# Rotary key of a latent-attention block: the low parts of its weights laid in the free columns beside the high parts, two matmul passes in place of three

## The chip, the cores and the metric

The kernel runs on one core of one Trainium2 chip. The metric is the device time of one execution in microseconds (us), as the median of several runs. Engines are named as the profile names them: PE is TensorE (matmuls), PEld its weight loads, DVE is VectorE, ACT is ScalarE, POOL is GpSimd, SP is SyncE, whose queue starts the DMAs.

## What is computed

The reference is a two-layer encoder over 512 tokens of width 1024. Each layer has three mixers side by side (latent attention, a gated linear recurrence in both directions, windowed attention), a gated merge, cross-attention and a gated feed-forward part. The change touches the shared rotary key of the latent attention alone. Cut to what matters:

```python
h = _rmsnorm(x, g_mix[l])
(a_cq, a_ckv, a_kr, b_q, b_ff, b_fb, ...) = _split_cols(h @ w_in[l], IN_SPLITS)   # a_kr: 32 columns

def _rope(x, pos):                       # x1, x2: the two halves of the 32 columns
    return concatenate([x1 * cos - x2 * sin, x1 * sin + x2 * cos])

k_rope = broadcast(_rope(a_kr, pos))     # one key of 32 columns, the same for all 8 heads
```

## The kernel before

**Precision.** All large products are kept near float32 by splitting each operand into a high part, rounded to the type fp32r, and a low part, the rest. `mm3` (line 153) issues three matmuls for a product of a weight block and an activation chunk: high by high, high by low, low by high. The fourth product, low by low, is left out.

**Weights.** All weights come as one stream of blocks of 128 x 128, four blocks to a unit. `_fetch` (L112) starts the DMA of a unit five ahead, `_part` splits a unit: ACT writes the high parts `whi` (L120), DVE subtracts and writes the low parts `wlo` (L121). `_next` does this so that a unit is parted two units before PE reads it (`LOOK = 3`). `blk` hands out the next block as a pair (high, low). Each tile `whi` and `wlo` holds 128 x 512 elements and there are five of each.

**The rotary key.** `mla_pre` makes a list of steps; the step `key` (line 574) multiplies the 1024 input features with a block of 128 columns, in eight chunks of 128 features (`kc`), so eight blocks, two units, 24 matmuls into one PSUM bank. The 32 wanted columns stand in the block twice, each time as themselves and as their two halves swapped: `[kr, krs, kr, krs]`. Two DVE instructions (L581) multiply the result by the tables of cosines and sines; the step `rope` (`turned`) sums the pairs by one matmul with a constant matrix of zeros and ones (`C_SWAP`) and splits the key.

**Where it stands.** The recurrence `hgrn` goes over eight heads, and its last two rounds carry the latent attention's first steps as filler for PE: in round `i == 6` the steps `ckv0`, `ckv1`, `key`, in that order, and in round 7 `cq0`, `nckv`, `cq1`, `rope`, `cq2`, `ncq`. Ahead of `key` in the same round stand the scores of head 6 (`hgrn_scores`), and in the round before `decay(heads[7])` was issued: some twenty DVE instructions for each direction (`hgrn_decay`, L410 to L463), part of them on ACT and POOL. Right after `key`, PE has the scores of head 7 (144 small matmuls), then `cq0`.

**What sets the order.** The tile framework orders each engine's instructions when the program is built: it puts waits on semaphores where a tile's region was written or read by another engine, and it may set an instruction behind later written ones of its engine. On the chip each engine's queue runs in that fixed order. Every layer runs the same code.

Of the kernel before, what the change touches and what calls it, by code (L numbers as in the profile page):

```python
# [9 lines left out]
F32 = mybir.dt.float32  # L10
# [6 lines left out]
P = 128  # L17
D = 1024
# [3 lines left out]
KC = D // P  # L22
# [22 lines left out]
C_M, C_ID, C_SWAP, C_BONE, C_SM = 0, 512, 640, 768, 896  # L45
# [3 lines left out]
def _consts():  # L49
    c = np.zeros((P, CTOT), np.float32)  # L50
    inv = (10000.0 ** (-np.arange(16, dtype=np.float32) / np.float32(16))).astype(np.float32)
    ang = np.arange(T, dtype=np.float32)[:, None] * inv[None, :]
    cos = np.cos(ang).T.astype(np.float32)
    sin = np.sin(ang).T.astype(np.float32)
    cs = np.concatenate([cos, cos, -sin, sin], 0)
    one = np.ones((64, T), np.float32)
    rope = np.stack([np.concatenate([one, cs], 0), np.concatenate([cs, one], 0)])
    t = np.arange(T)
    c[:, C_M:C_M + T] = (t % 16 != 0)
    c[:, C_ID:C_ID + P] = np.eye(P)  # L60
    p = np.arange(P)
    c[:, C_SWAP:C_SWAP + P] = (p[:, None] == p[None, :]) | (p[:, None] == (p[None, :] ^ 32))
    c[:, C_BONE:C_BONE + P] = ((p[:, None] // 64) == (p[None, :] // 64))
    j = np.arange(16)
    for i in range(4):
        n = 1 << i
        c[:, C_SM + 16 * i:C_SM + 16 * i + 16] = (j % n != 0)
        c[:, C_SM + 64 + 16 * (3 - i):C_SM + 80 + 16 * (3 - i)] = (j % n != 0)
    same = (p[:, None] // 32) == (p[None, :] // 32)
    mf = (~same) | (p[:, None] <= p[None, :])  # L70
    mb = (p[:, None] % 32) >= p[None, :]
    m = np.concatenate([mf, mb], 1).astype(np.int32)
    return c, m, rope


class _K:
# [479 lines left out]
    def mla_pre(self, l, h):  # L556

        nc = self.nc
        st = {"ckv": [], "cq": [], "acc": {}}

        def latent(nm, off, c):
            def run():
                if nm == "ckv" and c == 0:
                    st["rope"] = [self.t2(), self.t2()]
                    for e in range(2):
                        nc.sync.dma_start(st["rope"][e], self.roped[e])
                b, = self.projs("w_in", l, np.arange(D), [off + c * P + np.arange(P)], h)
                t = self.t2()
                nc.scalar.activation(t, b, AF.Copy)
                st["acc"][nm] = self.sumsq(t, st["acc"].get(nm))  # L570
                st[nm].append(t)
            return run

        def key():

            kr = O_KR + np.arange(32)
            krs = O_KR + np.concatenate([np.arange(16, 32), np.arange(16)])
            b, = self.projs("w_in", l, np.arange(D), [np.concatenate([kr, krs, kr, krs])], h)
            u = st["u"] = self.t2()
            for e, a in ((0, slice(64, 128)), (1, slice(0, 64))):  # L580
                nc.vector.tensor_tensor(u[a], b[a], st["rope"][e][a], op=ALU.mult)  # L581

        def norm(nm, n, g):
            def run():
                r = self.rstd(st["acc"][nm], n * P)
                st["n", nm] = [(self.t2(F32R), self.t2(F32R)) for _ in range(n)]
                self.norm_split(st[nm], V_N * l + g, r, st["n", nm])
            return run

        def turned():  # L590
            krr = self.bank()
            self.mm(krr, self.cst[:, C_SWAP:C_SWAP + P], st["u"], True, True)
            ktab = self.c8([P, 4, T], F32R)
            kt = st["kt"] = [(ktab[:, 0], ktab[:, 1]), (ktab[:, 2], ktab[:, 3])]
            for e in range(2):
                a = slice(64, 128) if e == 0 else slice(0, 64)
                self.split(kt[e][0][a], kt[e][1][a], krr[a])

        self.mst = st
        res = dict(key=key, rope=turned, nckv=norm("ckv", 2, V_GKV), ncq=norm("cq", 3, V_GQ))  # L600
        res.update({f"ckv{c}": latent("ckv", O_CKV, c) for c in range(2)})
        res.update({f"cq{c}": latent("cq", O_CQ, c) for c in range(3)})
        return res
# [519 lines left out]
def _layout(inp):  # L1123
    f = {k: np.asarray(v) for k, v in inp.items()}
    xT = np.ascontiguousarray(f["x"][0].T.reshape(KC, P, T).transpose(1, 0, 2))
    memT = np.ascontiguousarray(f["mem"][0].T.reshape(KC, P, M).transpose(1, 0, 2))
    cols = []
    for l in range(NL):
        for n in ("g_mix", "g_x", "g_mem", "g_ffn", "a_gq", "a_gkv"):
            cols.append(_cols(f[n][l]))  # L1130
        cols.append(np.tile(f["b_gout"][l], 2)[:, None])
        cols.append(np.tile(f["c_sink"][l][None], (P, 1)))
    cols.append(_cols(f["g_final"]))
    cols.append(_cols(f["b_lb"]))
    vec = np.ascontiguousarray(np.concatenate(cols, 1))
    assert vec.shape == (P, VTOT), vec.shape
    rel = np.arange(384)[None, :] - P - np.arange(P)[:, None]
    ext = np.concatenate([f["rel_bias"], np.full((1, 8), -1e30, np.float32)], 0)
    idx = np.where(np.abs(rel) <= 128, _t5_bucket(rel), 32)
    bias = np.ascontiguousarray(ext[idx].transpose(2, 0, 1))  # L1140
    cst, msk, rope = _consts()
    return dict(xT=xT, memT=memT, vec=vec, cst=cst, msk=msk, rope=rope, bias=bias)
# [37 lines left out]
```

## Time and profile before

| | |
|---|---|
| median of 3 runs | 2372.4 us (2371.82 to 2373.35) |
| the profiled execution's own time | 2371.25 us |
| its span in the profile | 2369.5 us |
| PE busy | 2336.9 us, 99% of the span |
| DVE busy | 1469.8 us, 62% |
| ACT busy | 1187.3 us, 50% |
| POOL busy | 167.8 us, 7% |

How to read it: the span goes from the first to the last instruction, the own time adds what lies around it. PE's busy time is the share of the span in which a matmul was under way; back-to-back matmuls overlap, so the mean duration of one is longer than the distance from one to the next. In a timeline row the first number is the start, the second how long the row's instructions took together, and a bracket at the end gives the idle time before and who ended it.

### The profile page before, as it was taken

The page shows a single profiled execution, that of the slowest core. Times are in us where ns is not written, and L with a number is a line of the kernel's source. Part 1 is how long each engine was busy: PE and PEld are TensorE (multiplying, and loading weights), DVE is VectorE, ACT ScalarE, POOL GpSimd, SP SyncE. Part 2 cuts the span into 40 slices and gives each one's busy share as a digit, 9 for nine tenths or more (in the row PEclk, how much of TensorE's full clock was granted, in tenths as well). Part 3 has the DMA queues.
Part 4 walks back from the last instruction along what each step waited for, and adds up shares of the span by engine and source line. Part 5 has one row for each costly group of instructions (what it writes and reads, how often), then busy time and mean ns, then how long its engine had stood idle before and what let it go on. Part 6 is the DMA issues. An engine that isn't in the chain of part 4 may idle for free.

```text
span 2369.5 us, 34666 instructions
## 1 busy us (share of the span) xinstructions
PE 2336.9 (99%) x12934; PEld 1901.6 (80%) x12934; DVE 1469.8 (62%) x2753; ACT 1187.3 (50%) x2162; POOL 167.8 (7%) x165
## 2 busy tenths in 40 slices
PE   9999999999999999999999999999999999999998
PEld 7877778777888888888887777777788888888886
DVE  8876756566756555355577866666657575553553
ACT  7766566556545433233367656655555454332332
POOL 1332300000000000000013322000000000000000
PEclk9999999999999999999999999999999999999999
DMA  4223233234553233333432223322345523333332
GB/s 163 86 86 94 84 96 103 80 98 134 196 148 89 80 94 98 98 96 96 130 106 87 84 69 102 98 85 91 95 140 178 147 76 94 94 98 98 96 96 76
DMA packets 133513, 246.26 MB, mean 104 GB/s; under 512 B 14816, under 2 KB 17120, under 8 KB 132960
## 3 DMA queue, kind: packets, MB, share of 16 engines
q1 hardware_dynamic: 133344, 244.05, 33.5%
q8 instruction: 101, 1.65, 0.3%
q14 instruction: 68, 0.56, 0.1%
HBM read 227.22 MB, written 16.78 MB: 103 GB/s over the span
## 4 chain that ended last, share of the span: by engine, by line
PE 85%; DVE 6%; issue 4%; POOL 2%; ACT 2%; DMA 1%; POOLq 0%; DVEq 0%; SPq 0%; ACTq 0%
PE ps L151 83%; POOL c L463 1%; PE ps L658 1%; DVE c L463 1%; DVE t L417 1%; POOL t L414 1%; DVE wlo L121 1%; DVE c L444 1%; PE ps L790 1%; DVE c L445 0%; ACT whi L120 0%; PE ps L939 0%; DMA t<-in_bias_dram 0%; DMA wraw<-in_w_dram 0%; PE ps L286 0%
## 5 line engine op out<-in xcount | busy, mean ns | idle before, releaser
L151 PE MATMUL ps<-c,whi 128*128 128x512 f32 (+1 forms) x5696 | 1733.9, 387 | 5.9 <-ACT whi L120 5.9
L151 PEld LDWEIGHTS ps<-c,whi 128*128 128x128 f32 x5696 | 1058.3, 188 | 236.8 <-issue 16.9
L151 PE MATMUL ps<-c,wlo 128*128 128x512 f32 (+1 forms) x2848 | 1096.9, 385 | 6.5 <-DVE wlo L121 6.5
L120 ACT ACTIVATE whi<-wraw 128x512 fp32r<-128x512 f32 x764 | 475.1, 629 | 817.3 <-PE ps L151 606.4
L121 DVE TENSOR_TENSOR wlo<-wraw,whi 128x512 fp32r<-128x512 f32 x764 | 526.5, 697 | 545.7 <-ACT whi L120 535.9
L151 PEld LDWEIGHTS ps<-c,wlo 128*128 128x128 f32 x2848 | 535.7, 188 | 116.2 <-DVE wlo L121 9.1
L151 PE MATMUL ps<-c,t 128*64 128x512 f32 (+6 forms) x960 | 167.5, 418 | 4.5 <-DVE smw L767 2.3
L151 PEld LDWEIGHTS ps<-c,t 128*64 128x64 f32 (+2 forms) x960 | 99.7, 167 | 55.3 <-issue 31.6
L988 DVE TENSOR_TENSOR t<-ps,t 128x512 f32<-128x512 f32 x112 | 76.3, 689 | 103.3 <-PE ps L151 103.3
L463 POOL TENSOR_TENSOR c<-c,smx 128x256 f32<-128x256 f32 x128 | 122.8, 988 | 111.0 <-DVE c L444 82.8
L414 POOL TENSOR_TENSOR t<-t,t 128x512 f32<-128x512 f32 x32 | 44.1, 1379 | 1184.4 <-ACT t L413 1169.0
L970 DVE TENSOR_TENSOR c<-ps,c 128x512 f32<-128x512 f32 x64 | 44.2, 690 | 70.1 <-PE ps L151 70.1
L463 DVE TENSOR_TENSOR c<-c,smx 128x256 f32<-128x256 f32 x128 | 81.6, 695 | 0.2
L151 PEld LDWEIGHTS ps<-c 128*32 128x32 f32 (+1 forms) x2304 | 61.2, 120 | 12.2 <-PE ps L151 5.3
L151 PE MATMUL ps<-c 128*32 128x32 f32 (+3 forms) x2304 | 69.3, 218 | 0.2
L180 ACT ACTIVATE c<-ps 128x512 fp32r<-128x512 f32 (+2 forms) x78 | 42.7, 547 | 39.9 <-PE ps L151 38.9
L181 DVE TENSOR_TENSOR c<-ps,c 128x512 fp32r<-128x512 f32 (+2 forms) x78 | 49.3, 632 | 20.8 <-ACT c L180 20.4
L441 ACT ACTIVATE t<-t 128x512 f32<-128x512 f32 x32 | 20.1, 629 | 79.7 <-DVE t L440 79.7
L417 DVE TENSOR_TENSOR_SCAN t<-cst,t 128x512 f32<-128x512 f32 x32 | 39.0, 1220 | 23.7 <-POOL t L414 23.7
L181 DVE TENSOR_TENSOR c<-t,c 128x512 fp32r<-128x512 f32 (+1 forms) x84 | 51.6, 634 | 3.3 <-ACT c L180 3.3
L180 ACT ACTIVATE c<-t 128x512 fp32r<-128x512 f32 (+1 forms) x84 | 48.0, 581 | 8.6 <-DVE t L982 3.5
L645 ACT ACTIVATE t<-ps,sm 128x512 f32<-128x512 f32 x64 | 43.5, 687 | 12.6 <-DVE sm L643 12.5
(144 smaller groups left out, 1788.2 us busy)
## 6 DMA issues: line engine op xcount, KB each, us to landing
wraw<-in_w_dram SPq DMA_DIRECT2D x764, 256.0 KB, 2.6
gate<-t SPq DMA_DIRECT2D x32, 256.0 KB, 2.3
t<-gate SPq DMA_DIRECT2D x32, 256.0 KB, 3.9
c<-in_xT_dram SPq DMA_DIRECT2D x16, 256.0 KB, 5.5
gate_b<-t SPq DMA_DIRECT2D x16, 256.0 KB, 3.4
t<-gate_b SPq DMA_DIRECT2D x16, 256.0 KB, 3.8
t<-in_bias_dram SPq DMA_DIRECT2D x16, 192.0 KB, 3.6
c<-in_memT_dram SPq DMA_DIRECT2D x3, 1024.0 KB, 8.2
```

Source lines behind the costliest of these rows:

```text
L120: self.nc.scalar.activation(hi, raw, AF.Copy)
L121: self.nc.vector.tensor_tensor(lo, raw, hi.bitcast(F32), op=ALU.subtract)
L151: self.nc.tensor.matmul(o, a, b, start=start, stop=stop)
L180: nc.scalar.activation(hi, src, AF.Copy)
L181: nc.vector.tensor_tensor(lo, src, hi.bitcast(F32), op=ALU.subtract)
L414: nc.gpsimd.tensor_tensor(f, f, g, op=ALU.add)
L417: scan = lambda o, m, x: nc.vector.tensor_tensor_scan(o, m, x, 0.0, op0=ALU.mult, op1=ALU.add)
L444: tt(qd, hd["q"], f, op=ALU.mult)
L463: eng.tensor_tensor(ov, sv, ev, op=ALU.mult)
L645: nc.scalar.activation(p, s, AF.Exp, bias=nm, accum_out=sm)
L970: nc.vector.tensor_tensor(x[c], b, xold[c], op=ALU.add)
L988: self.nc.vector.tensor_tensor(t, b, r, op=ALU.mult)
```

## The change

Line numbers of the changed kernel are the same up to `key` and 7 higher behind it.

```diff
-    c[:, C_SWAP:C_SWAP + P] = (p[:, None] == p[None, :]) | (p[:, None] == (p[None, :] ^ 32))
+    c[:, C_SWAP:C_SWAP + P] = (p[:, None] % 32 == p[None, :] % 32)
...
             kr = O_KR + np.arange(32)
             krs = O_KR + np.concatenate([np.arange(16, 32), np.arange(16)])
-            b, = self.projs("w_in", l, np.arange(D), [np.concatenate([kr, krs, kr, krs])], h)
+            cols = np.concatenate([kr, krs, kr, krs])
+            b = self.bank()
+            for kc in range(KC):
+                hi, lo = self.blk("w_in", l, np.arange(kc * P, (kc + 1) * P), cols)
+                nc.vector.tensor_copy(hi[:, 64:128], lo[:, 64:128].bitcast(F32))
+                for x in range(2):
+                    self.mm(b, hi, h[kc][x], kc == 0 and x == 0, kc == KC - 1 and x == 1)
```

In each of the eight blocks a DVE copy (a CAST in the lists below, L583) puts the low parts of the block's columns 64 to 127 over the high parts there. The block in `whi` then has high parts in columns 0 to 63 and low parts of the same weights in columns 64 to 127. It is multiplied with the high and the low part of the activations: two matmuls for each block, 16 in place of 24. The bank holds products of the high weights in rows 0 to 63 and of the low weights in rows 64 to 127, and the constant matrix now sums the four rows that belong to one output instead of two. The product low by low is now in the sum. The weight stream, its DMAs and its splitting are unchanged.

The program's order around the change, in the first layer (the second layer has the same rows under other numbers). `whi_3037` is the first unit of the key's weights, `whi_3055` the second, `ps_3076` the key's bank.

PE, the key's matmuls on the second unit (blocks 5 to 8), before:

```order
L151 MATMUL ps_3076<-c_44_221,whi_3055 128x512 [waits Activation_49]
L151 MATMUL ps_3076<-c_45_222,whi_3055 128x512
L151 MATMUL ps_3076<-c_44_221,wlo_3056 128x512 [waits DVE_49]
L151 MATMUL ps_3076<-c_44_221,whi_3055 128x512
L151 MATMUL ps_3076<-c_45_222,whi_3055 128x512
```

and now, to the first matmul of the scores of head 7:

```order
L151 MATMUL ps_3076<-c_44_221,whi_3055 128x512 [waits DVE_49,Activation_49]
L151 MATMUL ps_3076<-c_45_222,whi_3055 128x512
L151 MATMUL ps_3076<-c_44_221,whi_3055 128x512 [waits DVE_49]
L151 MATMUL ps_3076<-c_45_222,whi_3055 128x512
L151 MATMUL ps_3076<-c_44_221,whi_3055 128x512 [waits DVE_49]
L151 MATMUL ps_3076<-c_45_222,whi_3055 128x512
L151 MATMUL ps_3076<-c_44_221,whi_3055 128x512 [waits DVE_49]
L151 MATMUL ps_3076<-c_45_222,whi_3055 128x512
L151 MATMUL ps_3116<-c_494_2831 32x32 [waits PE_49]
```

Before, one wait for DVE's split covered the unit; now blocks 5, 6, 7 and 8 each wait for DVE on their own.

DVE, where the copies of the first unit and the first copy of the second unit stand now (the rows around them are those of before):

```order
L121 TENSOR_TENSOR wlo_3038<-wraw_2994,whi_3037 128x512 [waits DMAHW5_49,PE_49,Activation_49]
L411 TENSOR_SCALAR t_478_2768<-t_478_2768 128x512 [waits DVE_49]
L583 CAST whi_3037<-wlo_3038 128x64 [waits DVE_49]
L583 CAST whi_3037<-wlo_3038 128x64 x3
L492 COPY_PREDICATED zz_102<-msk_159,ps_2902 128x128 [waits PE_49]
...
L121 TENSOR_TENSOR wlo_3056<-wraw_3012,whi_3055 128x512 [waits DMAHW6_49,Activation_49]
L430 COPY smx_2872<-t_500_2870 128x16 [waits DVE_49]
L583 CAST whi_3055<-wlo_3056 128x64 [waits DVE_49,PE_49]
L431 TENSOR_TENSOR smx_2872<-smx_2872,t_500_2870 128x64 [waits DVE_49]
```

All four copies of the first unit follow that unit's split (L121) at once; of the second unit only the first copy does.

DVE, where the other three copies of the second unit stand, in the same queue, 21 instructions of other work later (the first ten, L431 to L396, are not shown):

```order
L463 TENSOR_TENSOR c_502_2885<-c_494_2831,smx_2872 128x256 [waits DVE_49]
L463 TENSOR_TENSOR c_502_2885<-c_494_2831,smx_2872 128x256 x3
L181 TENSOR_TENSOR c_154_825<-t_503_2894,c_153_824 128x512 [waits Activation_49]
L496 TENSOR_TENSOR c_506_2967<-zz_102 32x4x32 x4
L121 TENSOR_TENSOR wlo_3080<-wraw_3035,whi_3079 128x512 [waits DMAHW7_49,PE_49]
L121 TENSOR_TENSOR wlo_3098<-wraw_3053,whi_3097 128x512 [waits DMAHW0_49,Activation_49]
L583 CAST whi_3055<-wlo_3056 128x64 x3
L121 TENSOR_TENSOR wlo_3208<-wraw_3077,whi_3207 128x512 [waits DMAHW1_49,Activation_49]
L258 TENSOR_TENSOR t_520_3032<-t_520_3032,t_529_3073 128x512 [waits Activation_49]
```

The three copies that blocks 6, 7 and 8 wait for stand behind the end of head 7's decay (L463), the rest of head 6's scores (L496) and the splits of the next two units (the first two L121 rows), and ahead of the third.

## Rows read from the trace of the kernel before

**Rows 1.** Page, parts 1 and 2: busy us (share) xinstructions; granted clock in tenths.
```profile
PE 2336.9 (99%) x12934; PEld 1901.6 (80%) x12934; DVE 1469.8 (62%) x2753; ACT 1187.3 (50%) x2162; POOL 167.8 (7%) x165
...
PEclk9999999999999999999999999999999999999999
```

**Rows 2.** Page, part 5, costliest groups: busy, mean ns of one, idle before.
```profile
L151 PE MATMUL ps<-c,whi 128*128 128x512 f32 (+1 forms) x5696 | 1733.9, 387 | 5.9 <-ACT whi L120 5.9
...
L151 PE MATMUL ps<-c,wlo 128*128 128x512 f32 (+1 forms) x2848 | 1096.9, 385 | 6.5 <-DVE wlo L121 6.5
```

**Rows 3.** Waits of PE over the whole span: total us, times, longest us.
```profile
PE ps L151 <- DVE wlo L121: 6.5, 4, 2.3
PE ps L151 <- ACT whi L120: 5.9, 1, 5.9
PE ps L151 <- DVE t L258: 3.0, 2, 1.5
```

**Rows 4.** Timeline of PE, first layer: the key, head 7's scores, cq0.
```profile
282.19 0.62 PE L151 MATMUL ps<-c,whi 128*128 128x512 f32 x2
...
287.41 0.39 PE L151 MATMUL ps<-c,wlo 128*128 128x512 f32 x1
287.72 4.62 PE L151 MATMUL ps<-c 128*32 128x32 f32 x144
292.10 0.71 PE L151 MATMUL ps<-c,whi 128*128 128x512 f32 x2
```

**Rows 5.** Timeline of DVE, first layer, around the second key unit's split.
```profile
279.22 1.22 DVE L417 TENSOR_TENSOR_SCAN t<-cst,t 128x512 f32<-128x512 f32 x1 [1.18 <-POOL t L414]
280.36 0.67 DVE L121 TENSOR_TENSOR wlo<-wraw,whi 128x512 fp32r<-128x512 f32 x1
280.95 0.17 DVE L430 COPY smx<-t 128x16 f32<-128x16 f32 x1
281.15 0.28 DVE L431 TENSOR_TENSOR smx<-smx,t 128x64 f32<-128x64 f32 x1
...
286.86 2.16 DVE L496 TENSOR_TENSOR c<-zz 32x128 f32<-32x128 f32 x4
289.05 2.20 DVE L121 TENSOR_TENSOR wlo<-wraw,whi 128x512 fp32r<-128x512 f32 x3
...
292.48 1.41 DVE L581 TENSOR_TENSOR t<-ps,t 64x512 f32<-64x512 f32 x2
```

**Rows 6.** Timeline of DVE, first layer, behind the first key unit's split.
```profile
267.41 0.42 DVE L411 TENSOR_SCALAR t<-t 128x512 f32<-128x512 f32 x1
268.46 0.30 DVE L492 COPY_PREDICATED zz<-msk,ps 128x128 f32<-128x128 int32 x1 [0.63 <-PE ps L151]
```

**Rows 7.** Timelines of DVE and PE, second layer, the same place.
```profile
1463.31 2.20 DVE L121 TENSOR_TENSOR wlo<-wraw,whi 128x512 fp32r<-128x512 f32 x3
...
1461.99 4.62 PE L151 MATMUL ps<-c 128*32 128x32 f32 x144
```

**Rows 8.** Timeline of PE, first layer: head 6's scores and what follows.
```profile
267.12 4.30 PE L151 MATMUL ps<-c 128*32 128x32 f32 x144
271.18 0.71 PE L151 MATMUL ps<-c,whi 128*128 128x512 f32 x2
```

**Rows 9.** Chain that ended last, 280 to 300 us: start, us, what.
```profile
283.90 4.35 POOL c L463 x2
```

**Rows 10.** Stretches at the end: length, PE busy (x), PEclk, DMA share, GB/s.
```profile
2361.20:2362.70 1.50, 0.00 (x0) 1.00 0.00 0
2362.70:2364.20 1.50, 0.00 (x0) 0.55 0.98 378
```

**Rows 11.** Timeline of PE: its first matmuls, the twelfth's successor, its last ones.
```profile
5.88 1.22 PE L151 MATMUL ps<-c,whi 128*128 128x512 f32 x2 [5.88 <-ACT whi L120]
...
11.13 0.63 PE L151 MATMUL ps<-c,whi 128*128 128x512 f32 x2
...
2358.56 1.12 PE L151 MATMUL ps<-t,small 128*128 128x512 f32 x2 [0.59 <-ACT t L253]
```

## Prediction, made before the changed kernel was run

> **What bounds the kernel now.** I read the busy shares first, then the costliest groups, then PE's waits, and then the timelines of PE and DVE around the key. PE is busy 99% of the span at full granted clock [rows 1], nearly all of it in 128 x 512 matmuls on the weight stream [rows 2]. So a matmul that leaves PE's queue saves its distance to the next one, and a wait that is added to PE's queue is paid in full unless a wait further on shrinks by as much. PE's waits are few: apart from the start (5.9 us) the longest is 2.3 us, and that is for DVE's weight splits [rows 3]. DVE is busy only 62% over the span, but that is an average: from 279.22 to 293.9 us, in the stretch where the key stands, it has not one idle gap, working off head 7's decay; the first and the last row of that stretch, and the pieces that matter here, stand in [rows 5].
>
> **What is removed.** Eight matmuls a layer, those on `wlo`. The key's 24 matmuls start at 282.19 and the last starts at 287.41 [rows 4]: 5.22 us for 23 distances, 0.227 us each. 8 x 0.227 = 1.8 us a layer, 3.6 us for both. The bank, the two products with the tables, the one matmul with the constant matrix and the weight stream stay, at no cost either way: same instructions, same shapes, other numbers in them.
>
> **What is added.** Eight copies of 128 x 64 on DVE a layer. No row shows this operation. The nearest are the copy of 128 x 16, 0.17 us, and the two-input operation of 128 x 64, 0.28 us [rows 5]. The copy has the first one's operation and the second one's size; I take 0.2 us, with 0.1 and 0.28 as bounds (a negative price is excluded, since nothing is taken off DVE).
> The four copies of the first unit stand behind L411, which ends at 267.83, and ahead of a wait for PE that ended at 268.46 after 0.63 us of idle time [rows 6]. They need 0.8 us, so 0.2 us sticks out, and the next idle time takes it: DVE waits 1.18 us for POOL ahead of 279.22 [rows 5]. Their price is nothing; and PE reads this unit only at 282.19. If that idle time were gone, the price would be at most 0.8 us of DVE.
> The first copy of the second unit stands behind L430, at about 281.12, and delays all that follows on DVE by 0.2 us. Block 5 waits for it, at 282.19 + 8 x 0.227 = 284.0: hidden by almost 3 us.
>
> **The wait that decides.** The copies for blocks 6, 7 and 8 stand behind L496 and two weight splits. In the trace those splits begin at 289.05, three in 2.20 us, so two of them take 1.47 us and end at 290.52 [rows 5]. Add the 0.2 us of the first copy and 0.2 us for the copy itself: DVE delivers block 6 at about 290.95. PE wants it after ten matmuls, at 282.19 + 10 x 0.227 = 284.46. It will stand still for about 6.5 us. Nothing in DVE's queue up to there waits for PE's key, so DVE will not be later for it, nor earlier. The remaining copies follow at 0.2 us and a block lasts 0.45 us, so there is one stall, not three.
> Queued behind the stalled matmul on PE are the scores of head 7, `cq0` and everything after. The key's last matmul ends at 290.95 + 6 x 0.227 = 292.31 instead of 287.64: 4.67 us later, and the saved 1.8 us is in this number.
>
> **What comes back.** Head 7's scores take 4.38 us from their start to `cq0` [rows 4], but head 6's take 4.06 [rows 8]: in the trace they wait briefly for POOL, whose L463 ends at 288.25 [rows 9]. That wait will be over: 0.32 us back. Net 4.67 - 0.32 = 4.35 us a layer. DVE reaches the key's products (L581) at 292.48 anyway [rows 5], so they and what hangs on them are not later by more than about 1 us, and PE's next wait, 1.5 us for L258 near 322 us, is paced by PE's own matmuls ahead of it and moves along. The second layer has the same rows 1174.26 us later [rows 7], so I count everything twice: 8.7 us.
>
> **The clock.** A stall of 6.5 us has no like in the middle of this kernel. At its end it has: the last matmuls are over at 2359.7 [rows 11], the granted clock is still 1.00 up to 2362.7, and 0.55 in the next stretch, so it falls to 0.5, the 1.2 GHz level, about there, after PE has done nothing for some 3 us [rows 10]. And at the beginning the first 12 matmuls, after PE stood still for 5.88 us, take 11.13 - 5.88 = 5.25 us [rows 11], 0.44 each, where the same work takes 12 x 0.227 = 2.72 later: 2.5 us lost, at a spacing which I read as the lower level, though the page's clock row prints full clock there. By the waits in the middle alone (2.3 us at most, clock at full [rows 1, 3]) there would be no such loss and the sum would be 8.7 us; by the ends a stall that is more than twice as long as the silence before 2362.7 costs the clock too. I take the ends, and 2.5 us a layer, bounds 0 and 7.9: the upper one if the six matmuls left of the key (6 x 0.21 = 1.3 us), the whole of the scores (4.06 us more) and then another 2.5 us go at half speed.
> The Trainium skill, on the page "TensorE: Matmul & The Clock Gate", section "HAM oscillation — how this bites in real kernels", says that bursts of matmuls with waits between them start each burst at the halved clock once the waits are long enough. By that rule the sum would be the higher one; the mid-kernel waits of this trace neither confirm nor contradict it, as none is long, and the fall at the end agrees.
>
> **Sum.** Against the profiled execution's own 2371.25 us: 2371.25 + 8.7 + 2 x 2.5 = 2385.0 us. That execution lies 1.15 us below the median of the runs shown, well inside their spread. 0.2% of the time, 4.7 us, is about what a measurement of this kernel can tell from no change.
>
> **Rivals.**
> *The clock holds.* The stall is as computed, but PE restarts at full speed: 2371.25 + 8.7 = 2380.0. For it: no fall is seen between two matmuls anywhere in the span. Against it: the fall at the end.
> *The clock stays low through the scores.* The stage of 144 tiny matmuls keeps PE less occupied than the projections, and the clock may come back only in `cq0`: 2371.25 + 2 x (4.35 + 7.9) = 2395.8. For it: the trace has no row for this stage at the low clock. Against it: at full clock the same stage has never let the clock fall [rows 1].
> *The copies are in time, and it is not slower.* If DVE delivered block 6 by 284.46, only the 16 matmuls would be gone: 2371.25 - 3.6 = 2367.6. The point from which it decides is 6.5 us ahead of where the queue's order puts the copy, and DVE has no idle time between 280.36 and 290.5 to be taken out. What speaks for it is only that DVE's pace there may differ; it would have to finish 10 us of work in 3.5.
> *The stall is paid back later.* PE's longest later wait in a layer (1.5 us for L258 [rows 3]) would be shorter because DVE and ACT use the stall to get ahead. If the 1.5 us went and the clock held: 2371.25 + 2 x (4.35 - 1.5) = 2377.0. Against it: the work ahead of the L258 wait begins with a matmul result that is late by the same amount.
>
> **How the numbers follow.** Forecast, with the clock lost for a few us in one or both layers (2382 to 2388): 0.58. The clock holds: 0.20. Low through the scores: 0.12. Paid back: 0.06. Copies in time: 0.04. The range leaves out the copies in time and the edge of the outer cases: 2377 to 2396, from the paid-back case to the long low clock; the bounds of the copy's price, 0.2 us a layer, lie inside it. The copies in time (3.6 us faster) and about half of the paid-back case are within 0.2%: 0.07. Faster by more needs more than the removed matmuls are worth: 0.01. Slower: 0.92.
>
> **What would show it.** PE: 16 matmuls fewer; one wait of about 6.5 us in each layer put down to DVE's `whi` at L583, near 284.5 and 1458.7 us, inside the key; no wait of 0.3 us inside head 7's scores. DVE: the last three copies right behind two L121 rows at about 290.7. Clock: a dip in the stretch after 288 us and matmuls 0.43 apart for a few us. It is wrong if the three copies run before 285 us, if PE waits there for something else, if the rows after the stall are at full speed (then 2380), or if the waits after 295 us shrink by more than 1 us a layer.

## The result, and the profile after

The changed kernel takes 2387.21 us, the median of 5 runs (2383.16 to 2388.13), against 2372.8 us (5 runs) for the kernel before, run beside it: ratio 1.0056, 95% interval [1.0045, 1.0068]. It is slower by 14.4 us, 0.6%. The forecast was 2385.0 us, range 2377 to 2396, slower with a chance of 0.92. The prediction was right; the last sections say in which terms it was right for the right reason, and where errors met.

The profiled execution of the changed kernel took 2386.18 us, its span 2384.4 us, so it lies 14.9 us above that of before. Busy times hardly moved: PE issues 12918 matmuls, 16 fewer than in [rows 1], and is nevertheless busy for 2338.7 us, 1.8 us longer; DVE is busy for 1470.0 us, 62% as before. No share shows where 15 us went. PE's waits do (changed kernel, whole span: total us, times, longest us):

```profile
PE ps L151 <- DVE whi L583: 12.5, 2, 6.3
PE ps L151 <- DVE wlo L121: 6.0, 4, 2.3
PE ps L151 <- DVE t L258: 3.3, 3, 1.5
```

The first line is new, the others stand about as in [rows 3]. One wait of 6.3 us in each layer, for a copy at L583. Where it stands, the timeline of PE in the first layer shows (changed kernel; start, us, instruction, idle time before and who ended it), to be read beside [rows 4]:

```profile
283.23 2.43 PE L151 MATMUL ps<-c,whi 128*128 128x512 f32 x10
291.93 2.93 PE L151 MATMUL ps<-c,whi 128*128 128x512 f32 x6 [6.27 <-DVE whi L583]
294.79 4.30 PE L151 MATMUL ps<-c 128*32 128x32 f32 x144
298.84 0.71 PE L151 MATMUL ps<-c,whi 128*128 128x512 f32 x2
```

Ten matmuls, five blocks, at full speed; then 6.27 us of nothing; then the last six, which start 2.86 us before the scores, where 6 x 0.227 = 1.36 us would be their distance at the pace of the first ten. From the key's first matmul to the end of head 7's scores it is 298.84 - 283.23 = 15.61 us, where it was 292.10 - 282.19 = 9.91 us: +5.70. The second layer has the same rows, with a slower end (changed kernel, PE):

```profile
1464.62 2.43 PE L151 MATMUL ps<-c,whi 128*128 128x512 f32 x10
1473.31 2.93 PE L151 MATMUL ps<-c,whi 128*128 128x512 f32 x6 [6.26 <-DVE whi L583]
1476.17 5.53 PE L151 MATMUL ps<-c 128*32 128x32 f32 x144
1481.45 0.70 PE L151 MATMUL ps<-c,whi 128*128 128x512 f32 x2
```

In the kernel before, the same stage of the second layer begins and ends so (PE):

```profile
1456.46 0.62 PE L151 MATMUL ps<-c,whi 128*128 128x512 f32 x2
...
1466.37 0.70 PE L151 MATMUL ps<-c,whi 128*128 128x512 f32 x2
```

Here the stage takes 16.83 us instead of 9.91: +6.92. The scores themselves took 5.28 us from their start to the next matmul, in the first layer 4.05. The granted clock tells why (changed kernel, stretches of both layers, start and end in us: length, PE busy (matmuls), PEclk, DMA share, GB/s):

```profile
287.50:291.90 4.40, 0.00 (x0) 0.55 0.00 0
291.90:294.70 2.80, 2.77 (x6) 0.50 0.84 241
294.70:298.80 4.10, 4.10 (x144) 0.99 0.51 133
...
1473.30:1476.20 2.90, 2.89 (x10) 0.50 0.80 230
1476.20:1481.40 5.20, 5.20 (x144) 0.71 0.41 127
```

During the stall the clock falls to 0.50, the 1.2 GHz level. In the first layer it is back at full when the scores begin; in the second it comes back within them. The queue of DVE shows who is late (changed kernel, DVE, first layer; some rows left out), to be read beside [rows 5]:

```profile
268.80 0.49 DVE L583 CAST whi<-wlo 128x64 fp32r<-128x64 f32 x4
269.52 0.30 DVE L492 COPY_PREDICATED zz<-msk,ps 128x128 f32<-128x128 int32 x1 [0.22 <-PE ps L151]
...
282.19 0.20 DVE L583 CAST whi<-wlo 128x64 fp32r<-128x64 f32 x1
...
287.99 2.15 DVE L496 TENSOR_TENSOR c<-zz 32x128 f32<-32x128 f32 x4
290.18 1.59 DVE L121 TENSOR_TENSOR wlo<-wraw,whi 128x512 fp32r<-128x512 f32 x2
291.69 0.38 DVE L583 CAST whi<-wlo 128x64 fp32r<-128x64 f32 x3
```

The first unit's four copies run 14 us ahead of PE and go into idle time (0.63 us of it before [rows 6], 0.22 now). The second unit's first copy is also in time, its other three run at 291.69, between the second and third of the next units' splits, and PE starts again at 291.93.

The 14.9 us add up so: 1.04 us by which the key starts later (283.23 against 282.19; DVE's split of the key's first unit, which stands ahead of the first copies, already begins 1.05 us later, at 267.86 against 266.81, so this is no part of the change), 5.70 in the first layer, 1.42 between the layers (a clock fall of its own, last section), 6.92 in the second layer, -0.2 at the end. The two stages of the change give 12.6 us of it.

### The profile page after: what moved, and what is told of

It is laid out like the page before. It is cut to its first block, busy times and chain, and to the rows that moved or that the text cites. A ratio compares the mean times of both kernels' runs of the same rounds, so it can differ in the third digit from the quotient of the medians.

```text
span 2384.4 us, 34644 instructions
## 1 busy us (share of the span) xinstructions
PE 2338.7 (98%) x12918; PEld 1902.2 (80%) x12918; DVE 1470.0 (62%) x2769; ACT 1187.9 (50%) x2162; POOL 169.7 (7%) x165
## 4 chain that ended last, share of the span: by engine, by line
PE 84%; DVE 7%; issue 4%; ACT 2%; POOL 2%; DMA 1%; SPq 0%; DVEq 0%; POOLq 0%; ACTq 0%
PE ps L151 82%; PE ps L665 1%; DVE c L463 1%; POOL c L463 1%; DVE t L417 1%; DVE wlo L121 1%; POOL t L414 1%; DVE c L444 1%; PE ps L797 1%; DVE c L445 0%; DMA c<-in_memT_dram 0%; DVE c L496 0%; ACT whi L120 0%; PE ps L946 0%; DMA t<-in_bias_dram 0%
## 5 line engine op out<-in xcount | busy, mean ns | idle before, releaser
L121 DVE TENSOR_TENSOR wlo<-wraw,whi 128x512 fp32r<-128x512 f32 x764 | 526.5, 697 | 556.0 <-ACT whi L120 542.9
L463 POOL TENSOR_TENSOR c<-c,smx 128x256 f32<-128x256 f32 x128 | 124.8, 1003 | 111.2 <-DVE c L444 82.8
L463 DVE TENSOR_TENSOR c<-c,smx 128x256 f32<-128x256 f32 x128 | 80.3, 685 | 0.2
```

Source lines behind the costliest of these rows:

```text
L121: self.nc.vector.tensor_tensor(lo, raw, hi.bitcast(F32), op=ALU.subtract)
L463: eng.tensor_tensor(ov, sv, ev, op=ALU.mult)
```

## The experiments

The runs come in two sets, each on a chip of its own and each beside the kernel before (medians 2373.3 and 2373.09 us). Theory: DVE's queue place makes PE wait 6.3 us, and the clock makes it dearer. Rivals: the copies cost by the work that they are; the stall alone is the price; the matmuls saved are worth nothing.

**The stall filled.** Behind the fifth block of each key, and so ahead of the wait for the sixth, 26 matmuls whose result nobody reads:

```diff
+                if kc == 4:
+                    spare = self.bank()
+                    for _ in range(26):
+                        self.mm(spare, hi, h[kc][0], True, True)
```

> The changed kernel, with 26 more matmuls of 128x512 between block 5 and block 6 of the key, into a bank that nothing reads: work of 26 x 0.227 = 5.9 us a layer laid into the stall of 6.3 us. Theory (PE stands still there for a copy that DVE delivers late, and the clock falls because PE stands still): the matmuls cost nothing, the stall shrinks to some 0.4 us, no matmul behind it runs at the lower clock, and the time falls below that of the changed kernel: 2371.25 + 2 x 4.35 = 2380, plus at most 1.4 us where the clock falls elsewhere; 2380 to 2382. Rival (PE is simply slower by something else, the clock has no part in it): at least as slow as the changed kernel, 2386 to 2388, or, were there no stall to fill, 2386 + 11.8 = 2398.

Measured: 2380.82 us, median of 4 runs (2379.39 to 2385.58); ratio 1.0036 [1.0023, 1.005]. That is 6.4 us faster than the changed kernel by the medians of two sets, with 52 matmuls more; by the two ratios it is 0.0020, or 4.7 us, and their intervals overlap a little. Its size is better read from the stage. PE in the first layer, and its stretches:

```profile
284.75 8.32 PE L151 MATMUL ps<-c,whi 128*128 128x512 f32 x36
293.86 1.65 PE L151 MATMUL ps<-c,whi 128*128 128x512 f32 x6 [0.78 <-DVE whi L583]
295.44 4.30 PE L151 MATMUL ps<-c 128*32 128x32 f32 x144
299.50 0.70 PE L151 MATMUL ps<-c,whi 128*128 128x512 f32 x2
```

```profile
290.00:293.00 3.00, 3.00 (x14) 1.00 0.00 0
293.00:295.40 2.40, 1.62 (x7) 1.00 0.43 139
295.40:299.50 4.10, 4.10 (x146) 1.00 0.68 206
```

The last six matmuls still wait for L583, and PE does nothing useful in the same stretch, but the clock stays at 1.00 and they go at 1.58 us instead of 2.86. The stage takes 299.50 - 284.75 = 14.75 us, +4.84 on before; the second layer's takes 14.74. The wait is not quite the same one: PE goes on 9.11 us after the key's start (293.86 - 284.75), in the changed kernel 8.70 us, as DVE came 0.41 us later here.

So the extra time in the changed kernel can be taken apart. The clock takes 2.86 - 1.58 = 1.28 us from the last six matmuls in each layer, and 5.28 - 4.05 = 1.23 us from the scores of the second: 3.8 us. Without it the two stages are 5.70 - 1.28 = 4.42 and 6.92 - 2.51 = 4.41 us longer than before: that is the wait less the matmuls saved, 8.8 us. The difference of the medians from the kernel with the stall filled, 6.4 us, is larger than these 3.8; only one execution of each kernel has rows, and where the rest lies isn't shown. (The profiled execution of this run, 2385.58 us, is the slowest of the four; it lost clock at two other places, near 222 and 1403 us.)

**No copies at all.** The line with the copy is taken out, so the two passes see high parts alone and the products with the low weights are left out:

```diff
-                nc.vector.tensor_copy(hi[:, 64:128], lo[:, 64:128].bitcast(F32))
```

> The changed kernel without its eight copies a layer: two passes on the high parts alone, so the product of the low weights is left out. It shows what the removal of the 16 matmuls is worth by itself. Theory: nothing or little, since PE now reaches the scores of head 7 at 285.9 instead of 287.7, and the same chain of DVE, ACT and POOL (its L463 ended at 288.25 in the kernel before) releases them: a wait of about 2.1 us for POOL in place of 0.3; 2372 to 2373. Rival (each matmul that leaves the queue saves its 0.227 us, as the forecast priced it): 2372.4 - 3.6 = 2368.8.

Measured: 2372.65 us, 11 runs (2368.26 to 2375.89); ratio 0.9996 [0.9987, 1.0005]. The whole loss is gone, but no gain can be told from zero, though 16 matmuls are gone; the 3.6 us that they would be worth lie just outside the interval. PE in the two layers:

```profile
283.52 3.79 PE L151 MATMUL ps<-c,whi 128*128 128x512 f32 x16
287.24 0.76 PE L151 MATMUL ps<-c 128*32 128x32 f32 x28
288.42 4.03 PE L151 MATMUL ps<-c 128*32 128x64 f32 x116 [0.42 <-DVE c L463]
292.20 0.70 PE L151 MATMUL ps<-c,whi 128*128 128x512 f32 x2
...
1457.76 3.79 PE L151 MATMUL ps<-c,whi 128*128 128x512 f32 x16
1463.23 0.36 PE L151 MATMUL ps<-c 128*32 128x32 f32 x10 [1.38 <-POOL c L463]
1463.86 4.05 PE L151 MATMUL ps<-c 128*32 128x64 f32 x116 [0.27 <-POOL c L463]
1467.66 0.70 PE L151 MATMUL ps<-c,whi 128*128 128x512 f32 x2
```

The key ends 1.8 us earlier, as it should, and the scores behind it then wait for the decay of their own head (L463). In the first layer the stage is 8.68 us, 1.23 less than before; in the second 9.90 against 9.91: the saving is spent there in full on two waits for POOL, 1.38 and 0.27 us.

**The copies, unread.** The kernel before, with the same copies into a tile of their own that nobody reads:

```diff
...
+                nc.vector.tensor_copy(scratch, lo[:, 64:128].bitcast(F32))
+                self.mm3(b, (hi, lo), h[kc], kc == 0, kc == KC - 1)
```

> The kernel before, all three passes, with the eight copies a layer added at the place of the change but into a tile that nothing reads, so that no matmul waits for them. Theory (the copies as work cost nothing, the wait for them does): 2372.4 plus at most 0.2 us a layer, as the first copy of the second unit delays head 7's decay by 0.1 to 0.2 us; 2372 to 2373. Rival (DVE is short of time there and its load costs): 8 x 0.2 us a layer and more, 2375 or above.

Measured: 2373.66 us, 10 runs (2370.89 to 2375.19); ratio 1.0002 [0.9993, 1.0011]. As work on DVE the copies cost nothing that can be told from zero; the interval leaves room for 2.6 us at most. As nothing waits for them, the last three stand a little later in DVE's queue than in the changed kernel, singly at 292.14, 292.84 and 293.55 us. What costs is that PE reads them.

**The low parts made in place.** No copy; in the split of the key's two units DVE writes the low parts of columns 64 to 127 straight into `whi`, where the high parts would have stood:

```diff
+        if u in (82, 83, 464, 465):
+            ...
+            self.nc.scalar.activation(h4[:, :, 0:64], r4[:, :, 0:64], AF.Copy)
+            self.nc.vector.tensor_tensor(h4[:, :, 64:128], r4[:, :, 64:128], h4[:, :, 0:64].bitcast(F32),
+                                         op=ALU.subtract)
+            self.units[u] = (hi, hi)
...
-                nc.vector.tensor_copy(hi[:, 64:128], lo[:, 64:128].bitcast(F32))
```

> The changed kernel without any copy: for the key's units ACT rounds only columns 0 to 63 of each block and DVE subtracts straight into columns 64 to 127 of the same tile, so two passes see the same weights as in the changed kernel and DVE has less work. But in DVE's queue this split of the second unit stands behind L496, where the late copies stood one place further on. Theory (the place in DVE's queue costs, not the copies): PE stops at block 5, at 284.0, until the split is done at 289.05 + 0.4 = 289.5, a stall of about 5.5 us, 291.3 instead of 287.6 at the key's end, less 0.3 for POOL, plus 1 to 2.5 us for the clock: 4.4 to 5.9 us a layer, 2381 to 2384. Rival (the copies cost): without them 2368.8 to 2372.4.

Measured: 2383.89 us, 4 runs (2382.87 to 2386.05); ratio 1.0044 [1.0029, 1.006]. Without one copy in the program, PE waits as in the changed kernel (PE, first layer, then the DVE row that it waits for):

```profile
282.74 1.98 PE L158 MATMUL ps<-c,whi 128*128 128x512 f32 x8
289.72 3.75 PE L158 MATMUL ps<-c,whi 128*128 128x512 f32 x8 [5.00 <-DVE whi L122]
```

```profile
288.85 0.72 DVE L122 TENSOR_TENSOR whi<-wraw,whi 128x256 fp32r<-128x256 f32 x1
```

The split of the second unit itself has come to stand behind L496, so block 5 waits 5.00 us. It isn't the copy but the place in DVE's queue: work for PE's next matmuls stands behind a backlog. This was no cure. In the second layer the wait at this place, 5.41 us, is put down to ACT's `whi` (L127), but DVE's split of the unit stands there too and ends at 1472.66 us, just ahead of the matmul at 1472.81.

**The key one round later.** The changed kernel, with the steps `key` and `cq0` exchanged, so that the key no longer stands right ahead of head 7's scores:

```diff
-                for nm in ("ckv0", "ckv1", "key"):
+                for nm in ("ckv0", "ckv1", "cq0"):
...
-                for nm in ("cq0", "nckv", "cq1", "rope"):
+                for nm in ("key", "nckv", "cq1", "rope"):
```

> The changed kernel, copies included, with the steps key and cq0 exchanged: cq0 stands in round 6, the key in round 7 behind the scores of head 7 and a gate projection, where DVE's queue has the key's splits and copies well ahead of the matmuls that want them. Theory: no stall for the copies, and PE comes to the scores of head 7 no earlier than in the kernel before, so no longer wait for POOL; the 16 matmuls fewer are now worth 16 x 0.227 = 3.6 us: 2372.4 to 2373.3 (the kernel before) less 3.6, that is 2368.8 to 2369.7. Rival 1 (copies between a split and its matmuls always stall PE): 2380 or more. Rival 2 (what follows is set by DVE, ACT and POOL again, so a shorter key is worth nothing): as before, 2372 to 2373.

Measured: 2369.26 us, 11 runs (2365.46 to 2374.96); before on the same chip 2373.09 (27 runs); ratio 0.9987 [0.9979, 0.9996]. It is the fastest kernel of the study, by 3.8 us; that is 0.16%, less than the 0.2% that the prediction named as what can be told from no change, and the interval lies just below 1. DVE's last copies, then PE, in the first layer:

```profile
294.66 0.50 DVE L583 CAST whi<-wlo 128x64 fp32r<-128x64 f32 x4
```

```profile
288.71 4.32 PE L151 MATMUL ps<-c 128*32 128x32 f32 x144
292.78 0.71 PE L151 MATMUL ps<-c,whi 128*128 128x512 f32 x2
...
298.32 3.79 PE L151 MATMUL ps<-c,whi 128*128 128x512 f32 x16
301.95 1.02 PE L151 MATMUL ps<-t,small 128*128 128x512 f32 x2
```

All eight copies are done by 295.2 us and PE wants them from 298.32 on: no wait for L583 is left.

**The same exchange, three passes.** The kernel before with `key` and `cq0` exchanged in the same way.

> The kernel before, three passes and no copies, with key and cq0 exchanged in the same way: the control for the kernel key_later. Theory: the same time as the kernel before, within 1 us, so the gain of key_later is the removed matmuls and not the exchange. Rival: the exchange itself brings 2 us or more.

Measured: 2374.13 us, 11 runs (2371.31 to 2376.14); ratio 1.0006 [0.9997, 1.0014]. The exchange alone gives nothing. So the gain of the run above belongs to the two passes: 2374.13 - 2369.26 = 4.9 us between the medians, where 16 matmuls at 0.227 us are 3.6. In the first layer, from the scores' start to the matmul behind the key, it is 15.07 us with three passes and 301.95 - 288.71 = 13.24 with two: 1.83 us, which is 8 x 0.227.

**Both remedies.** The key one round later, and its low parts made in place.

> The kernel key_later without copies: for the key's units ACT rounds only half of the columns and DVE subtracts straight into the other half. Theory: as key_later, 2368.8 to 2369.7, since the copies are hidden there anyway; fewer DVE and ACT microseconds give nothing. Rival: copies or splits still cost something there, and it is faster than key_later by 1 us or more.

Measured: 2372.42 us, 11 runs (2368.23 to 2375.64); ratio 0.9995 [0.9986, 1.0004]: nothing gained, and the expectation (2368.8 to 2369.7) is missed. In its trace a wait elsewhere is longer, for a table of biases that a DMA brings (L780; in the kernel before this wait, there at L767, is 1.01 us at the same place):

```profile
514.23 4.53 PE L158 MATMUL ps<-c,t 128*64 128x256 f32 x16 [3.33 <-DVE smw L780]
```

DVE itself waits 4.44 us for that DMA; the two transfers of biases near there take 5.3 us from issue to landing, 3.1 us in the kernel before (medians of two). Why, and whether this is the whole of the lost gain, stays open.

**The third pass put back.** The changed kernel with its copies and waits, but three passes in the loop (the low products then count twice):

```diff
-                for x in range(2):
-                    self.mm(b, hi, h[kc][x], kc == 0 and x == 0, kc == KC - 1 and x == 1)
+                self.mm3(b, (hi, lo), h[kc], kc == 0, kc == KC - 1)
```

> The changed kernel with its copies and its waits, and the third pass put back (the matmul on the low parts; the sum then holds some products twice, so the output is not the reference's). Theory: 5 of the 8 matmuls a layer stand ahead of the stall and only shorten it, 6.3 us to about 5.2; the 3 behind it cost 3 x 0.227 = 0.68 us a layer: 1.4 us over the changed kernel, 2387 to 2389. Rival (each of the 16 matmuls counts): 3.6 us over it, 2390 to 2391. Should the shorter stall cost less clock, the time may lie 1 to 2 us lower in both.

Measured: 2389.93 us, 4 runs (2388.63 to 2390.95); ratio 1.0075 [1.0061, 1.0089]: 2.7 us over the changed kernel. That is between the two expectations and nearer to the rival's, 2390 to 2391, so the time alone doesn't decide. PE's wait does (whole span):

```profile
PE ps L151 <- DVE whi L583: 10.9, 2, 5.5
```

Five more matmuls now run ahead of the stall, 5 x 0.227 = 1.1 us, and it is 5.46 and 5.45 us long instead of 6.27 and 6.26: they were put into the time that PE waits, less 0.3 us by which DVE was later. The other three come behind the stall, at the low clock, and lengthen the six matmuls' 2.86 us to 4.13 and 4.14: 1.27 us a layer, where 3 x 0.227 = 0.68 were expected. So the two stages are 3.2 us longer than in the changed kernel, 2.5 by these three matmuls and 0.7 by the later DVE. So of the eight matmuls that the change saves in a layer, five only made the stall longer, as the theory has it.

## Why the prediction was right, point by point

- **The place in the queue** decided, as predicted. "It will stand still for about 6.5 us": 6.27 and 6.26. The trace of before gave the start of the splits, and the program's order the place of the copies behind them.
- **The price of a copy**, 0.2 us between bounds of 0.1 and 0.28: 0.18 to 0.20 for one alone, four in a row in 0.49 us. The first unit's copies went into idle time, and in the run with unread copies no cost of their work can be told from zero.
- **The wait less what is saved and comes back**, 4.35 us a layer, 8.7 in all: 4.42 and 4.41 us, 8.8 in all, when the clock's share is taken out of the two stages. This term was right, and for the reason given.
- **The clock**, 2.5 us a layer, 5.0 in all: 1.3 us in the first layer and 2.5 in the second, 3.8 in all. The mechanism was right, the size too large in one layer: the row that the term was sized by was the start of the kernel, where the low clock lasted 12 matmuls; here it lasted six, and in the second layer about a third of the scores' work. The rule of the Trainium skill that the prediction weighed (page "TensorE: Matmul & The Clock Gate", section "HAM oscillation — how this bites in real kernels"), by which a burst behind a long enough wait starts at the halved clock, is borne out by the stretches of both layers.
- **The sum** of 2385.0 against 2386.18 us of the profiled execution is nearer than its terms deserve. In the execution 2.5 us are no part of the change (1.04 ahead of the key, 1.42 between the layers), and the two layers together gave 12.6 us where 13.7 were forecast. That these 2.5 us made up for a clock term 1.2 us too large is luck.
- **Two readings** were off, with no weight in the sum. The prediction's own terms for the sixth block, 290.52 and twice 0.2, give 290.92 and not 290.95 us. And 288.25 us is the end of the second of POOL's four instructions at L463, which the chain in [rows 9] names; all four last 5.59 us and end at 289.49.
- **The rival "the copies are in time"** was priced wrongly, at 2367.6 us. Its step says that "only the 16 matmuls would be gone"; with the copies taken out PE's queue is the same, and the time is 2372.65. The prediction used POOL's L463 for the 0.32 us that would come back, and not for what the row also says: head 7's scores are released by the decay's last step, on POOL and, as the run without copies shows, on DVE, so behind a key that ends earlier they only wait longer. Even without a stall the change could have gained little at this place: 1.23 us in one layer of the profiled execution, nothing in the other. The rule "a matmul that leaves PE's queue saves its distance to the next one" was put without an exception; the one named behind it, a wait further on, was given for an added wait alone and holds for a removed matmul too.
- **The clock holds, the clock stays low through the scores, the stall is paid back**: none of them came. The second layer was part of the way to the second, with the scores at a mean clock of 0.71; but the clock came back within them, and not in the matmuls behind. The waits for L258 stand at 3.3 us in all, against 3.0, so nothing was paid back there.
- A name was wrong, there and in the section on the kernel before: what PE does behind head 7's scores is the projection of a gate and then `cq0`. No number hangs on it.

## What to carry to other kernels

Before adding an instruction that the next matmul needs, look at the producing engine's queue in the program's order and at when the rows ahead of it end; a mean busy share of 62% said nothing about a stretch with no gap. A saved matmul is worth its distance only if the next wait of the same engine isn't released by somebody else; moving the shortened step behind that wait brought the saving here, and the same edit went from +14.4 us to -3.8 us. A stall in the middle of PE's work can cost more than its length: add what the clock takes after it, here 1.3 and 2.5 us behind stalls of 6.3 us.

## What was not expected of the hardware

**The clock falls behind a short wait in some executions and not in others.** The changed kernel has this between the layers, away from the change (PE's rows, then stretches):

```profile
1397.94 0.61 PE L151 MATMUL ps<-c,whi 128*128 128x512 f32 x2
1400.80 0.79 PE L151 MATMUL ps<-c,wlo 128*128 128x512 f32 x1 [2.25 <-DVE wlo L121]
```

```profile
1398.00:1400.00 2.00, 0.55 (x3) 1.00 0.00 0
1400.00:1402.00 2.00, 1.20 (x3) 0.68 0.12 20
1402.00:1404.00 2.00, 2.00 (x7) 0.50 1.01 288
```

The kernel before has the same wait, and in its profiled execution the clock stayed at 1.00 behind it (before, PE):

```profile
1394.15 0.50 PE L151 MATMUL ps<-c,wlo 128*128 128x512 f32 x1 [2.25 <-DVE wlo L121]
```

The nine matmuls from the end of the wait on take 3.71 us in the changed kernel and 2.18 in the kernel before: the fall costs 1.5 us. Every kernel of this study has such a wait for a weight split, once near 220 and once near 1400 us. In the ten profiled executions the clock fell behind it eight times: six times in twelve at a wait of about 2.25 us, twice in eight at one of about 1.85. Which it will be wasn't found out. Of the 48 runs of the kernel before in the two sets, those whose mean granted clock is given as 0.999 took 2369.5 to 2373.2 us, those with 0.997 took 2373.5 to 2376.8, and those with 0.998 lie between and across. So falls of the clock go with much of the spread between runs; that these waits are where they happen isn't shown, as those runs have no rows.

**DVE and POOL share the last step of the decay unevenly, and not always the same way.** The last four instructions of the decay on each of the two engines (L463), in the two layers of the kernel without copies:

```profile
285.23 3.52 POOL L463 TENSOR_TENSOR c<-c,smx 128x256 f32<-128x256 f32 x4 [4.71 <-ACT t L569]
...
1459.46 5.59 POOL L463 TENSOR_TENSOR c<-c,smx 128x256 f32<-128x256 f32 x4 [4.71 <-ACT t L569]
```

```profile
286.67 2.69 DVE L463 TENSOR_TENSOR c<-c,smx 128x256 f32<-128x256 f32 x4
...
1460.47 1.42 DVE L463 TENSOR_TENSOR c<-c,smx 128x256 f32<-128x256 f32 x4
```

Where one engine's four are shorter the other's are longer: 3.52 and 2.69 us, or 5.59 and 1.42. Which it will be was seen to change between layers and between kernels. In the kernel without copies it went with what the saved matmuls brought: 1.23 us in the layer of the first kind, where PE waits for DVE, and nothing in the other, where it waits for POOL. In the runs with the stall filled and with the third pass, POOL's row is 3.51 or 3.52 us in the first layer, and there the late copies came 0.41 and 0.33 us later. What decides it wasn't tried.
